# Two rows of the first chunk in banks of another ring, first reads in another order

## The chip, the cores and the metric

The kernel runs on one core of a Trainium2 chip. The metric is device time in microseconds (us) of the whole program. Engines are named as in the profile: PE is TensorE (PEld its weight loads), DVE is VectorE, ACT is ScalarE, POOL is GpSimd and SP is SyncE, which here only issues DMAs.

## The reference

One step of a decoder trunk with two layers, on 1024 prompt tokens and 8 x 4 sample tokens, 1056 in all, with a model width of 1024. The first layer is an RG-LRU block (width 1536), the second an HGRN2 block; both begin with an RMS norm and an input projection and end with an output projection and a residual. All is in float32. Cut to what the change touches:

```python
def _rmsnorm(x, gain):
    y = xf * lax.rsqrt(jnp.mean(xf * xf, axis=-1, keepdims=True) + EPS)
    return y * gain

def _lru_layer(x, g_norm, w_in, conv_w, conv_b, w_r, b_r, w_i, b_i, lam, w_out, h0, buf):
    xn = _rmsnorm(x, g_norm)
    u = xn @ w_in                                  # 1024 x 3072
    xb, gate = u[..., :W_LRU], u[..., W_LRU:]
    xc, new_buf = _causal_conv(xb, conv_w, conv_b, buf)
    h, h_last = _rg_lru(xc, w_r, b_r, w_i, b_i, lam, h0)
    y = h * silu(gate)
    return x + y @ w_out, h_last, new_buf

def _trunk(x, ...):
    x, h, bf = _lru_layer(x, ...)                  # layer 0
    x, S = _hgrn_layer(x, ...)                     # layer 1
    return _rmsnorm(x, final_gain), h, bf, S
```

## The kernel before

**Tiles.** The activations lie transposed: features on the 128 partitions, tokens along the rows. The 1056 tokens are three chunks of 352 (`CH`). A *row* of a projection is 128 output features: `product` makes it for one chunk out of eight blocks of 128 input features. A float32 product is made of three fast matmuls (`mm3`, L291 to L293): x and w are split into a rounded high part and the rest (`xh`, `xl`; `whi`, `wlo`), and hi x hi, lo x hi and hi x lo are added up in one PSUM bank. So a row of one chunk is 24 matmuls. ACT makes the high parts (L436 for weights, L956 for x), DVE or POOL subtract for the rest (L379, L957).

**Banks.** PSUM has eight banks in two rings of four: `mm` for the products of the projections, `hg` for the small matmuls beside them (gates of the recurrence L647/L651, sums and broadcasts of the norm). `next(mm)` takes the next bank of the ring, and a product that takes a bank has to wait until what lay in it has been read.

**The start.** The first six rows, three of the gate and three of the convolution branch (`items`), are computed chunk by chunk, with all their weights loaded at the start: rows one and two of the first chunk together (`pair`), then three to six. The norm of the first two chunks (`UN`) isn't applied to x: the products are made of x times the gain, and when a bank is read, L611 or L551 multiply by a broadcast of the root of the norm, `bcs[c]`. `by_token` makes that: it reads the chunk's tokens once more, with tokens on the partitions (`xt`, three reads into tiles `R`), ACT squares and sums them (L511), DVE and POOL take the root (L512, L518), DVE puts it on a diagonal (L519, L522), PE spreads it over the partitions (L524), ACT copies it (L965). Until the first data are there PE runs `WARM` small matmuls (L813).

**The order of the work.** Every operation is recorded with `fl.add`: engine, an assumed duration, what it reads and writes, a priority. `Flow.run` plans the order of each engine from these, first by list scheduling and then by `search`, which tries random changes and keeps those that make the planned end no later: `SEARCH` tries for what lies in the first 60 us or so, and then a part of that number for the whole layer. The instructions are then issued in this order, and each engine runs its own in order. `pin` fixes the order of the first DMAs: the reads with smaller numbers come first in SP's queue. The products of the projections keep their order among themselves (`main=True`); the small matmuls are put between them by the plan. The two layers are planned one after the other.

Of the kernel before, what the change touches and what calls it, by code (L numbers as in the profile page):

```python
# [19 lines left out]
ALU = mybir.AluOpType  # L20
PSUM = bass.MemoryType.PSUM
KB = 5
WARM = 32
SEARCH = 3000
NW, NXO, NRAW = 4, 3, 3
K1 = 5
NMM = 3
# [14 lines left out]
CH = 352  # L42
# [9 lines left out]
class Flow:  # L52
# [180 lines left out]
    def run(self, tries=0, first=0.0):  # L233
        self.after = [[] for _ in self.ops]
        for i, o in enumerate(self.ops):
            for d in o[3]:
                self.after[d].append(i)
        best = got = self.plan([o[4] for o in self.ops])
        for _ in range(self.TURNS):
            got = self.plan(self.back(got[2], got[4]))  # L240
            self.ends.append(got[0])
            best = min(best, got, key=lambda g: g[0])
        if tries:
            best = self.search(self.search(best, tries, first), tries // 2, 1e6)
        self.log = [(i, self.ops[i][0], best[1][i], best[2][i]) for i in best[3]]
        for i in best[3]:
            self.ops[i][2]()
# [12 lines left out]
def tile_trunk(ctx: ExitStack, tc: tile.TileContext, xT, xt, prm, hc, w0, wg, wo0, w1, wo1, s_in,  # L260
# [86 lines left out]
    with ExitStack() as l0:  # L347
# [10 lines left out]
            return cycle([(psum.tile([128, 512], F32, tag=tag, bufs=n, name=tag), (tag, i)) for i in range(n)])  # L358

        def dma(dst, src, r=(), w=(), prio=5, kb=180, q=Q):  # L360
            fl.add("SP" if q is Q else "ACT", 0.45, lambda: q.dma_start(dst, src), r, w, prio, kb * (1.0 if r or fl.exact else 0.75))

        def pin(*at):

# [79 lines left out]

            return get

        def product(w, xs, step=8, more=()):

            ps, pk = next(mm)
            n = len(xs)  # L450
            for s in range(0, n, step):
                ks = range(s, min(n, s + step))

                def emit(ks=ks):
                    for k in ks:
                        mm3(ps[:, :CH], w(k)[:2], *xs[k][:2], k == 0, k == n - 1)

                fl.add("PE", (0.484 if fl.exact else 0.48) * len(ks), emit, (*(q for k in ks for q in (*xs[k][2], *w(k)[2])), *more), (pk,), 1, main=True)
            return ps, pk

        def xcols(c):
# [41 lines left out]
        def by_token(c, prio):  # L503

            r, rk = next(nrs)
            dve(4, lambda: V.memset(r, 1.0), (), (rk,), 0)
            for i, (a, u) in enumerate(spans(CH)):
                t, tk = next(spots)
                dma(t[:u], xt[c * CH + a:c * CH + a + u], (), tk, prio, 4 * u * 0.75)
                pin((3, 8, 10)[c], i)  # L510
                act(D, lambda t=t, u=u, i=i: S.activation(junk[0][:u], t[:u], AF.Square, accum_out=r[:u, i:i + 1]), tk, (*junk[1], rk), prio, 0.06)  # L511
            dve(3, lambda: V.tensor_scalar(r[:, :3], r[:, :3], 1.0 / D, EPS, op0=ALU.mult, op1=ALU.add), (rk,), (rk,), 0)  # L512
            return spread(r, rk, next(xrs))
# [107 lines left out]
        def lru(g):  # L621
# [11 lines left out]
            for c in range(NCH):  # L633
# [5 lines left out]
                for i, hb in ((0, hbr), (1, hbi)):  # L639
                    for j in range(3):  # L640
                        m = 3 * g + j
                        ps, pk = next(hg)
                        (a, ak), (b, bk) = xpart(j, 0, c), xpart(j, 1, c)
                        u = 3 * i + j
                        fl.add("PE", 0.48, lambda ps=ps, a=a, b=b, u=u: mm3(ps[:, :CH], (gh[:, u, :], gl[:, u, :]), a, b, True, True),
                               (ak, bk, ("gh", u // 4 * 4), ("gl", u // 4 * 4)), (pk,), 0)
                        act(CH, lambda ps=ps, R=R, i=i, j=j, hb=hb, m=m: S.activation(R[:, i, j], ps[:, :CH], AF.Tanh, bias=hb[:, m:m + 1],  # L647
                                                                           scale=0.5), (pk, ("sm",)), (("R", s, i, j),), 2, 0.05)
                    ps, pk = next(hg)

                    fl.add("PE", 0.62, lambda ps=ps, i=i, c=c: T.matmul(ps[:96, :CH], gs[:, i, :], ST[:96, chunk(c)], start=True, stop=True),  # L651
                           (("gs",), *(("ST", j, c) for j in range(3))), (pk,), 0)
                    act(CH, lambda ps=ps, i=i: S.activation(td[:, i], ps[:96, :CH], AF.Tanh, bias=hbd[:96, 4 * i + g:4 * i + g + 1],
                                                            scale=0.5), (pk, ("sm",)), (("td", i),), 2, 0.05)
                    for j in range(3):
                        w = slice(32 * j, 32 * j + 32)
                        dma(R[w, i, j], td[w, i], (("td", i),), (("R", s, i, j),), 2, 45)
# [289 lines left out]
        def begin(c, first, last):  # L947

            for i in range(first, last):
                ws.append(weights(items[i][0], 1024, (0, 1, 1.2, 1.6, 1.7, 1.8)[i], V if i in VI else G, homes[i], Q if i else S, raw1[i], (-1, 0, 2, 4, 5, 7)[i]))  # L950
            for k, (x, xk) in enumerate(raw[c]):
                dma(x, xT[k][:, chunk(c)], (), (xk,), (0, 1.4, 1.9)[c])
                pin(0.001 if (c, k) < (0, 2) else (1, 6, 9)[c], k)
                if c in UN:
                    a, b = xh[k][:, chunk(c)], xl[k][:, chunk(c)]
                    act(CH, lambda x=x, a=a, k=k: S.activation(a, x, AF.Copy, scale=g0s[k]), (xk, ("g0",)), (("xh", k, c),), 1)  # L956
                    dve(CH, lambda x=x, a=a, b=b, k=k: V.scalar_tensor_tensor(b, x, g0s[k], a.bitcast(F32), op0=ALU.mult, op1=ALU.subtract),  # L957
                        (xk, ("g0",), ("xh", k, c)), (("xl", k, c),), 1, True)
                if c not in BYTOK:
                    squares(k, x, xk, accs[c], V, sqs)  # L960
            if c == 0:
                dma(hct, hc, (), (("hct",),), 2, 196)
            bc, bk = by_token(c, (1.25, 1.65, 2.0)[c]) if c in BYTOK else norm(accs[c], next(xrs))
            if c in UN:
                act(CH, lambda bc=bc: S.copy(bcs[c][0], bc), (bk,), (bcs[c][1],), 0)  # L965
            else:
                for k, (x, xk) in enumerate(raw[c]):
                    scaled_parts(c, k, x, xk, bc, bk, g0s[k], ("g0",), G if k % 4 == 3 else V)

        def products(c):  # L970
# [3 lines left out]
                    items[i][1](c, *got, bcs[0])  # L974
                order = order[2:]
            for i in order:
                items[i][1](c, *product(ws[i], xcols(c), 1, more=later[i]), *(bcs[c:c + 1] if c in UN else []))

        def pair(ws, xs):

            got = [next(mm) for _ in ws]
            for k, (a, b, ks) in enumerate(xs):
                for w, (ps, pk) in zip(ws, got):
                    fl.add("PE", 0.48, lambda ps=ps, w=w, k=k, a=a, b=b: mm3(ps[:, :CH], w(k)[:2], a, b, k == 0, k == KD - 1),
                           (*ks, *w(k)[2]), (pk,), 1, main=True)
            return got

# [933 lines left out]
```

## Time and profile before

| | |
|---|---|
| median of 3 runs | 1049.08 us (1048.25 to 1051.23) |
| the profiled execution | 1046.86 us |
| its span, first to last instruction | 1044.9 us |
| PE busy | 1030.1 us, 99% of the span |
| DVE, ACT, POOL busy | 78%, 55%, 49% |
| granted TensorE clock, mean | 0.997 |
| DMA engines' share, 10 to 20 us and 40 to 50 us | 0.97 and 0.50 |

The profile is that of one execution. Matmuls are pipelined and overlap in its rows, so the step from one start to the next is what one of them costs PE. In the list of waits, and in brackets behind a row of the timeline, stand the engine's idle time and what is taken to have ended it; the instruction named is the last that ended before, which need not be the one that was needed. In rows of windows stand the busy time of each engine with its number of records, then the granted clock, the share of the 16 DMA engines and the GB/s they moved.

### The profile page before, as it was taken

The page shows a single profiled execution, that of the slowest core. Times are in us where ns is not written, and L with a number is a line of the kernel's source. Part 1 is how long each engine was busy: PE and PEld are TensorE (multiplying, and loading weights), DVE is VectorE, ACT ScalarE, POOL GpSimd, SP SyncE. Part 2 cuts the span into 40 slices and gives each one's busy share as a digit, 9 for nine tenths or more (in the row PEclk, how much of TensorE's full clock was granted, in tenths as well). Part 3 has the DMA queues.
Part 4 walks back from the last instruction along what each step waited for, and adds up shares of the span by engine and source line. Part 5 has one row for each costly group of instructions (what it writes and reads, how often), then busy time and mean ns, then how long its engine had stood idle before and what let it go on. Part 6 is the DMA issues. An engine that isn't in the chain of part 4 may idle for free.

```text
span 1044.9 us, 25535 instructions
## 1 busy us (share of the span) xinstructions
PE 1030.1 (99%) x9810; PEld 1000.3 (96%) x9810; DVE 817.5 (78%) x1622; ACT 572.0 (55%) x1276; POOL 512.9 (49%) x596
## 2 busy tenths in 40 slices
PE   9999999999999999999999999999999999999997
PEld 9899999999999999999999999999999999999986
DVE  5889797889789679555588997988979797995436
ACT  6576746865764875334345464646463645652324
POOL 0225354454535456644527655555555555552544
PEclk9999999999999999999999999999999999999998
DMA  9701212223751686553655141423324242577204
GB/s 300 224 17 53 58 48 75 58 54 110 234 171 52 187 257 182 173 186 112 191 151 162 55 163 61 129 87 112 106 93 133 80 138 85 182 220 215 87 1 167
DMA packets 93210, 135.00 MB, mean 129 GB/s; under 512 B 11776, under 2 KB 70144, under 8 KB 93088
## 3 DMA queue, kind: packets, MB, share of 16 engines
q1 hardware_dynamic: 83296, 116.97, 36.4%
q10 hardware_dynamic: 9792, 16.40, 5.0%
q8 instruction: 77, 1.26, 0.5%
q14 instruction: 45, 0.37, 0.1%
HBM read 90.26 MB, written 38.20 MB: 123 GB/s over the span
## 4 chain that ended last, share of the span: by engine, by line
PE 66%; DVE 6%; issue 2%; DMA 1%; POOL 1%; ACT 1%; POOLq 0%; SPq 0%; DVEq 0%; ACTq 0%
PE mm L291 18%; PE mm L292 18%; PE mm L293 18%; PE hg L1161 2%; PE hg L1375 1%; PE hg L1377 1%; DVE R L1143 1%; DVE sg L1143 1%; PE hg L1419 1%; PE hg L1323 1%; DVE R L1544 1%; PE mm L1323 1%; DVE a L1343 0%; PE hg L1246 0%; PE hg L651 0%
## 5 line engine op out<-in xcount | busy, mean ns | idle before, releaser
L291 PE MATMUL mm<-xh,whi 128*128 128x352 f32 (+1 forms) x1127 | 351.7, 312 | 0.4 <-DVE k L1607 0.4
L293 PE MATMUL mm<-xh,wlo 128*128 128x352 f32 (+1 forms) x1127 | 347.6, 308 | 0.0
L292 PE MATMUL mm<-xl,whi 128*128 128x352 f32 (+1 forms) x1127 | 347.4, 308 | 0.0
L379 POOL TENSOR_TENSOR wlo<-wraw,whi 128x256 fp32r<-128x256 f32 (+3 forms) x188 | 209.1, 1128 | 191.9 <-ACT whi L1534 78.9
L291 PEld LDWEIGHTS mm<-xh,whi 128*128 128x128 f32 x1127 | 211.8, 188 | 2.7 <-DVE k L1607 1.0
L292 PEld LDWEIGHTS mm<-xl,whi 128*128 128x128 f32 x1127 | 212.2, 188 | 1.5 <-DVE xl L379 0.2
L293 PEld LDWEIGHTS mm<-xh,wlo 128*128 128x128 f32 x1127 | 212.0, 188 | 0.0
L291 PE MATMUL mm<-t,whi 128*128 128x264 f32 (+1 forms) x330 | 96.5, 292 | 0.8 <-DVE k L1607 0.8
L292 PE MATMUL mm<-t,whi 128*128 128x264 f32 (+1 forms) x330 | 94.4, 286 | 0.0
L293 PE MATMUL mm<-t,wlo 128*128 128x264 f32 (+1 forms) x330 | 94.3, 286 | 0.0
L576 DVE SCALAR_TENSOR_TENSOR k<-xb,prm_sb,k 128x352 f32<-128x352 f32 (+2 forms) x144 | 89.2, 626 | 4.4 <-ACT k L573 1.2
L379 POOL TENSOR_TENSOR wlo<-R,whi 128x256 fp32r<-128x256 f32 x70 | 66.1, 964 | 34.9 <-ACT whi L1534 19.9
L1607 DVE TENSOR_TENSOR k<-mm,k 128x264 f32<-128x264 f32 x154 | 64.0, 423 | 16.0 <-PE mm L293 14.8
L666 POOL TENSOR_TENSOR k<-X 128x352 f32<-128x352 f32 x36 | 43.0, 1199 | 59.5 <-DVE R L667 47.1
L291 PEld LDWEIGHTS mm<-t,whi 128*128 128x128 f32 x330 | 62.0, 188 | 1.6 <-DVE k L1607 1.0
L293 PEld LDWEIGHTS mm<-t,wlo 128*128 128x128 f32 x330 | 62.1, 188 | 0.0
L292 PEld LDWEIGHTS mm<-t,whi 128*128 128x128 f32 x330 | 62.1, 188 | 0.0
L436 ACT CAST whi<-wraw 128x512 fp32r<-128x512 f32 (+2 forms) x79 | 43.4, 571 | 20.0 <-PE mm L292 13.9
L291 PE MATMUL mm<-yh,whi 128*128 128x352 f32 x153 | 51.1, 334 | 0.6 <-DVE k L718 0.6
L293 PE MATMUL mm<-yh,wlo 128*128 128x352 f32 x153 | 49.4, 323 | 0.0
L647 ACT ACTIVATE R<-hg,smalls 128x352 f32<-128x352 f32 x72 | 38.2, 550 | 20.4 <-DVE R L687 11.0
L292 PE MATMUL mm<-yl,whi 128*128 128x352 f32 x153 | 49.4, 323 | 0.0
(454 smaller groups left out, 2501.5 us busy)
## 6 DMA issues: line engine op xcount, KB each, us to landing
wraw<-in_w_dram SPq DMA_DIRECT2D x52, 256.0 KB, 3.0
wraw<-in_w_dram ACTq DMA_DIRECT2D x37, 256.0 KB, 3.0
wraw<-in_wo_dram SPq DMA_DIRECT2D x34, 192.0 KB, 2.5
R<-in_w_dram ACTq DMA_DIRECT2D x17, 256.0 KB, 3.5
sg<-in_xT_dram SPq DMA_DIRECT2D x24, 176.0 KB, 4.3
si<-in_s_in_dram SPq DMA_DIRECT2D x8, 512.0 KB, 6.2
vt<-sg SPq DMA_DIRECT2D x8, 512.0 KB, 3.1
sg<-vt SPq DMA_DIRECT2D x32, 128.0 KB, 2.8
```

What stands on the lines that cost most here:

```text
L291: T.matmul(out, wh, xh, start=first, stop=False)
L292: T.matmul(out, wh, xl, start=False, stop=False)
L293: T.matmul(out, wl, xh, start=False, stop=last)
L379: emit = lambda: e.tensor_tensor(b, x, a.bitcast(F32), op=ALU.subtract)
L436: act(m, lambda hi=hi, raw=raw, m=m: S.copy(hi[:, :m], raw[:, :m]), rk, (hk,), prio)
L576: dve(u, lambda src=src, dst=dst, sh=sh, k=k: V.scalar_tensor_tensor(dst, sh(src, k), pc("cw", 12 * k + m), dst, op0=ALU.mult, op1=ALU.add ...
L647: act(CH, lambda ps=ps, R=R, i=i, j=j, hb=hb, m=m: S.activation(R[:, i, j], ps[:, :CH], AF.Tanh, bias=hb[:, m:m + 1], scale=0.5), (pk, ("s ...
L666: pool(CH, lambda x=x, a=a, b=b: G.tensor_tensor(x, a.bitcast(F32), b.bitcast(F32), op=ALU.add), (ak, bk), (xk,), 3)
L1143: dve(n // 2, lambda sv=sv, dv=dv, s=s, f=f: V.tensor_tensor(dv[:, :, s, :], sv[:, :, s, :], f, op=ALU.mult), (*sk, *gk), dk if i == o els ...
L1161: T.matmul(ps[32 * j:32 * j + 32, n * w:n * w + w], B[:, o:o + 32], q(slice(o, o + 32)), start=True, stop=True, tile_position=(0, 32 * j))
L1323: T.matmul(ps[:, n * 128:(n + 1) * 128], kt[:, 4 * i + n, :], vt[:, 4 * i + n], start=True, stop=True)
L1607: dve(QT, lambda: V.tensor_tensor(o[0], z[0], u[0], op=ALU.add), (z[1], u[1]), (o[1],), 0)
```

## The change

- Rows five and six of the first chunk take their banks from `hg` instead of `mm` (`product` gets a `ring`). All later products take the `mm` banks in turn, as before.
- The first reads are pinned in another order: row four's weights ahead of the first chunk's token reads, row six's weights ahead of the second chunk's x.
- `WARM` goes from 32 to 36, `SEARCH` from 3000 to 5000, the second part of the search from a half to a sixth of it (1500 to 833 tries).
- The planner reckons 0.482 us for three matmuls, where it had 0.48, and 0.87 or all of a first read's size, where it had 0.75.

```diff
-WARM = 32
-SEARCH = 3000
+WARM = 36
+SEARCH = 5000
...
-            best = self.search(self.search(best, tries, first), tries // 2, 1e6)
+            best = self.search(self.search(best, tries, first), tries // 6, 1e6)
...
-            fl.add("SP" if q is Q else "ACT", 0.45, lambda: q.dma_start(dst, src), r, w, prio, kb * (1.0 if r or fl.exact else 0.75))
+            fl.add("SP" if q is Q else "ACT", 0.45, lambda: q.dma_start(dst, src), r, w, prio, kb * (1.0 if r or fl.exact else 0.87))
...
-        def product(w, xs, step=8, more=()):
+        def product(w, xs, step=8, more=(), ring=None):
 
-            ps, pk = next(mm)
+            ps, pk = next(ring or mm)
...
-                fl.add("PE", (0.484 if fl.exact else 0.48) * len(ks), emit, (*(q for k in ks for q in (*xs[k][2], *w(k)[2])), *more), (pk,), 1, main=True)
+                fl.add("PE", (0.484 if fl.exact else 0.482) * len(ks), emit, (*(q for k in ks for q in (*xs[k][2], *w(k)[2])), *more), (pk,), 1, main=True)
...
-                dma(t[:u], xt[c * CH + a:c * CH + a + u], (), tk, prio, 4 * u * 0.75)
-                pin((3, 8, 10)[c], i)
+                dma(t[:u], xt[c * CH + a:c * CH + a + u], (), tk, prio, 4 * u)
+                pin((4, 8, 10)[c], i)
...
-                ws.append(weights(items[i][0], 1024, (0, 1, 1.2, 1.6, 1.7, 1.8)[i], V if i in VI else G, homes[i], Q if i else S, raw1[i], (-1, 0, 2, 4, 5, 7)[i]))
+                ws.append(weights(items[i][0], 1024, (0, 1, 1.2, 1.6, 1.7, 1.8)[i], V if i in VI else G, homes[i], Q if i else S, raw1[i], (-1, 0, 2, 3, 5, 6)[i]))
...
-                pin(0.001 if (c, k) < (0, 2) else (1, 6, 9)[c], k)
+                pin(0.001 if (c, k) < (0, 2) else (1, 7, 9)[c], k)
...
-                items[i][1](c, *product(ws[i], xcols(c), 1, more=later[i]), *(bcs[c:c + 1] if c in UN else []))
+                items[i][1](c, *product(ws[i], xcols(c), 1, later[i], None if c or i < 4 else hg), *(bcs[c:c + 1] if c in UN else []))
```

The other two places with 0.48 for three matmuls change as the first does. In what follows the instructions stand as the built programs have them, with the numbers of their tiles.

On PE, in the first chunk, before: the end of row three (`mm_160`, weights in `X`), the broadcast L524 and the beginning of row four (`mm_161`, weights in `yh0`).

```order
L291 MATMUL mm_160<-xh_109,X_144 128x352
L292 MATMUL mm_160<-xl_110,X_144 128x352
L293 MATMUL mm_160<-xh_109,X_144 128x352
L524 MATMUL hg_163<-k_87,ones_80 128x352
L291 MATMUL mm_161<-xh_95,yh0_152 128x352
L292 MATMUL mm_161<-xl_96,yh0_152 128x352
L293 MATMUL mm_161<-xh_95,yl0_155 128x352
```

And after, the end of row four, the same broadcast, and the beginning of row five (weights in `yh1`):

```order
L291 MATMUL mm_161<-xh_109,yh0_152 128x352
L292 MATMUL mm_161<-xl_110,yh0_152 128x352
L293 MATMUL mm_161<-xh_109,yl0_155 128x352
L524 MATMUL hg_163<-k_87,ones_80 128x352
L291 MATMUL hg_165<-xh_95,yh1_153 128x352
L292 MATMUL hg_165<-xl_96,yh1_153 128x352
L293 MATMUL hg_165<-xh_95,yl1_156 128x352
```

The broadcast has moved behind row four, and row five goes to `hg_165` (row six to `hg_162`); before, row five went to `mm_158`, the bank of row one.

In SP's queue, the first reads, before: weights in `a`, `ST` and `wraw`, the first chunk's tokens in `R` (from `in_xt`), and the beginning of the second chunk's x in `sg` (from `in_xT`).

```order
L361 DMA a_114<-in_w0_dram 128x512
L361 DMA a_115<-in_w0_dram 128x512
L361 DMA R_73<-in_xt_dram 128x1024 x2
L361 DMA R_73<-in_xt_dram 96x1024
L361 DMA a_115<-in_w0_dram 128x512
L361 DMA ST_145<-in_w0_dram 128x512
L361 DMA wraw_121<-in_w0_dram 128x512
L361 DMA wraw_122<-in_w0_dram 128x512
L361 DMA sg_146<-in_xT_dram 128x352
```

And after, from the same read on:

```order
L361 DMA a_114<-in_w0_dram 128x512
L361 DMA a_115<-in_w0_dram 128x512 x2
L361 DMA ST_145<-in_w0_dram 128x512
L361 DMA R_73<-in_xt_dram 128x1024 x2
L361 DMA R_73<-in_xt_dram 96x1024
L361 DMA wraw_121<-in_w0_dram 128x512
L361 DMA wraw_122<-in_w0_dram 128x512
L361 DMA ST_145<-in_w0_dram 128x512
L361 DMA sg_146<-in_xT_dram 128x352
```

Row four's weights (the second read into `a_115` and the first into `ST_145`) have moved ahead of the tokens, and the first half of row six's (the second into `ST_145`) ahead of the second chunk's x. Further on, not shown, the second chunk's token reads stand behind all of the third chunk's x and the reads of `gs`, `hct` and one block into `xo`; before, they stood among and ahead of these.

On DVE, in the second chunk, before: the third chunk's root (L512) and its diagonal (L519, L522; `nr0`), and the first bank that is read, L611 on `mm_158`.

```order
L512 TENSOR_SCALAR nr0_132<-nr0_132 128x3
L494 MEMSET nr1_133 128x4
L582 TENSOR_TENSOR X_144<-k_87,X_144 128x352
L576 SCALAR_TENSOR_TENSOR k_87<-xb_2_136,prm_sb_74,k_87 128x352
L519 TENSOR_TENSOR k_87<-ident_75,nr0_132 128x256
L522 TENSOR_SCALAR k_87<-ident_75,nr0_132 128x96
L494 MEMSET nr0_132 128x4
L860 RECIPROCAL smalls_84<-smalls_84 128x8
L582 TENSOR_TENSOR X_144<-k_87,X_144 128x352
L860 TENSOR_TENSOR smalls_84<-smalls_84 128x8 x4
L860 TENSOR_SCALAR smalls_84<-smalls_84 128x8
L611 TENSOR_TENSOR sg_147<-mm_158,xo_1_138 128x352
```

And after, the second chunk's root and diagonal (`nr1`), the third chunk's, and L611 on the bank of the second chunk's first row, which is `mm_158` now:

```order
L512 TENSOR_SCALAR nr1_133<-nr1_133 128x3
L582 TENSOR_TENSOR X_144<-k_87,X_144 128x352 x2
L519 TENSOR_TENSOR k_87<-ident_75,nr1_133 128x256
L522 TENSOR_SCALAR k_87<-ident_75,nr1_133 128x96
L494 MEMSET nr1_133 128x4
L512 TENSOR_SCALAR nr0_132<-nr0_132 128x3
L519 TENSOR_TENSOR k_87<-ident_75,nr0_132 128x256
L611 TENSOR_TENSOR sg_148<-mm_158,xo_1_138 128x352
L611 TENSOR_TENSOR sg_147<-mm_160,xo_1_138 128x352
```

L611 follows L519 directly. On PE the second chunk's L524 has moved towards that chunk's fifth row, which takes the bank of its first: 38 rows of PE's order lay between them before, 13 now. The last 5,159 instructions of PE, which begin shortly before the second layer, have the same order before and after.

More of the change, by code (lines that the diff above doesn't have):

```diff
@@ L644, in lru @@
                         u = 3 * i + j
-                        fl.add("PE", 0.48, lambda ps=ps, a=a, b=b, u=u: mm3(ps[:, :CH], (gh[:, u, :], gl[:, u, :]), a, b, True, True),
+                        fl.add("PE", 0.482, lambda ps=ps, a=a, b=b, u=u: mm3(ps[:, :CH], (gh[:, u, :], gl[:, u, :]), a, b, True, True),
                                (ak, bk, ("gh", u // 4 * 4), ("gl", u // 4 * 4)), (pk,), 0)
@@ L983, in pair @@
                 for w, (ps, pk) in zip(ws, got):
-                    fl.add("PE", 0.48, lambda ps=ps, w=w, k=k, a=a, b=b: mm3(ps[:, :CH], w(k)[:2], a, b, k == 0, k == KD - 1),
+                    fl.add("PE", 0.482, lambda ps=ps, w=w, k=k, a=a, b=b: mm3(ps[:, :CH], w(k)[:2], a, b, k == 0, k == KD - 1),
                            (*ks, *w(k)[2]), (pk,), 1, main=True)
```

## The prediction

> **What bounds the kernel now.** I read the page's head first, then the list of waits of TensorE, then the engine timelines at the places that the waits name.
>
> ```profile
> span 1044.9 us, 25535 instructions
> PE 1030.1 (99%) x9810; PEld 1000.3 (96%) x9810; DVE 817.5 (78%) x1622; ACT 572.0 (55%) x1276; POOL 512.9 (49%) x596
> ...
> PE mm L291 <- DVE nr L506: 2.1, 1, 2.1
> PE hg L1215 <- DVE R L1143: 1.6, 1, 1.6
> PE mm L291 <- DVE k L1607: 1.1, 2, 0.8
> PE hg L813 <- DVE nr L506: 1.0, 1, 1.0
> PE hg L1789 <- DVE sg L1779: 0.8, 1, 0.8
> PE mm L291 <- DVE k L718: 0.6, 1, 0.6
> PE hg L291 <- ACT R L647: 0.3, 1, 0.3
> ...
> PE hg L524 <- DVE k L522: 0.2, 1, 0.2
> ```
>
> PE (TensorE) is busy for 1030.1 of 1044.9 us, so the time changes only by work added to PE and by its waits. In each row of waits the first number is the total. Those of the first layer are 2.1 (fifth row of the first chunk), 0.2 (the broadcast of L524), 0.6 and 0.3 (L718, L647, late in that layer); 1.0 is the start. The order of PE's last 5,159 instructions, the whole second layer among them, is the same before and after, so I leave 1.6, 1.1 and 0.8 as they are. What the change can win is thus a little over 3 us, 0.3% of the time, which is also about what a measurement of this kernel can tell from no change.
>
> The start and the two waits in the timeline of PE (start, duration, instruction):
>
> ```profile
> 1.03 9.04 PE L813 MATMUL hg<-ones 128*128 128x128 f32 x64 [1.03 <-DVE nr L506]
> 9.82 0.41 PE L291 MATMUL mm<-xh,whi 128*128 128x352 f32 x1
> ...
> 21.34 0.32 PE L293 MATMUL mm<-xh,X 128*128 128x352 f32 x1
> 21.82 0.86 PE L524 MATMUL hg<-k,ones 128*128 128x352 f32 x2 [0.16 <-DVE k L522]
> 22.25 0.59 PE L291 MATMUL mm<-xh,yh 128*128 128x352 f32 x1
> 22.67 0.32 PE L292 MATMUL mm<-xl,yh 128*128 128x352 f32 x1
> ...
> 26.19 0.32 PE L293 MATMUL mm<-xh,yl 128*128 128x352 f32 x1
> 28.57 0.42 PE L291 MATMUL mm<-xh,yh 128*128 128x352 f32 x1 [2.06 <-DVE nr L506]
> 28.83 0.32 PE L292 MATMUL mm<-xl,yh 128*128 128x352 f32 x1
> ...
> 36.36 0.32 PE L291 MATMUL mm<-xh,X 128*128 128x352 f32 x1
> ```
>
> Records of PE overlap, so I work with the step from one start to the next. The wait at 28.57 is named after a memset, but what ends it is the emptying of the first bank:
>
> ```profile
> 22.78 3.47 ACT L956 ACTIVATE xh<-sg,g 128x352 fp32r<-128x352 f32 x7
> ...
> 27.18 0.44 ACT L965 COPY xo<-hg 128x352 f32<-128x352 f32 x1
> ...
> 28.00 0.96 DVE L611 TENSOR_TENSOR sg<-mm,xo 128x352 f32<-128x352 f32 x2
> ```
>
> The four `mm` banks hold rows one to four. The fifth needs bank one, whose L611 needs the copied broadcast of L965, which stands behind seven L956 on ACT; L611 starts at 28.00, and PE 0.57 later.
>
> **The change part by part.**
>
> *Two rows in the other ring.* The fifth and sixth row no longer wait for L611. The steps give the price: from 26.19 to 28.83 are 2.64 us for two steps. An ordinary step is 0.16 (48.05 to 48.21 in the next fence), so two take 0.32, and 2.32 us go. What is late next is the bank of chunk two's first row. It starts near 34.6 (below) and finds bank one emptied if L611 ends by then; in after's order L611 stands behind all eight of chunk two's xl. L611's 28.00 leaves 6 us for that. The reads of rows five's and six's weights have as many bytes ahead of them as before, or fewer.
>
> *The broadcast after the fourth row.* L524 waited for its input; an undisturbed one tells its own cost:
>
> ```profile
> 48.05 0.32 PE L292 MATMUL mm<-xl,yh 128*128 128x352 f32 x1
> 48.21 0.32 PE L293 MATMUL mm<-xh,yl 128*128 128x352 f32 x1
> 48.37 0.75 PE L524 MATMUL hg<-k,ones 128*128 128x352 f32 x2
> 48.69 0.59 PE L291 MATMUL hg<-X,gh 128*128 128x352 f32 x1
> 49.12 0.32 PE L292 MATMUL hg<-X,gh 128*128 128x352 f32 x1
> ```
>
> From the last matmul ahead of it to the second behind it: 49.12 - 48.21 = 0.91. At the first broadcast it is 22.67 - 21.34 = 1.33. The difference, 0.42 us, goes if the input is there in time. It comes later now: two reads of 256 KB (row four's weights, 128x512 of four bytes) stand ahead of the token reads, 0.524 MB.
>
> ```profile
> 21.50 0.26 DVE L522 TENSOR_SCALAR k<-ident,nr 128x96 f32<-128x96 f32 x1
> 10.00:26.50 16.50, 16.34 (x99) 15.57 (x97) 10.07 (x23) 12.93 (x28) 0.86 (x1) 1.00 1.01 331
> ```
>
> The DMA engines were full there (share 1.01) at 331 GB/s, so 1.6 us later: 21.76 becomes 23.4. PE reaches L524 near 26.2, so 2.8 us cover it; without that cover the 0.42 would come back and grow.
>
> *Four more warm-up matmuls.* Each is two records. The mean of 9.04 us over 64 would be 0.141 a record and 1.13 us for eight. But the records are not alike:
>
> ```profile
> 1.00:5.00 4.00, 3.97 (x21) 1.00 0.81 253
> 5.00:9.00 4.00, 4.00 (x38) 1.00 1.00 324
> ```
>
> Early ones take about 0.2 us, later ones 4.00/38 = 0.105 to 4.00/36 = 0.111 (two records may only reach in). The added ones come at the end, so they cost eight times the later price: 0.84 to 0.89, I take 0.87. The column PEclk says 1.00 in both windows and would not have told this. The Trainium skill, "TensorE: Matmul & The Clock Gate", Part 1: The HAM clock gate, says that the array starts at half rate and is released after some 3.4 us of work, so that matmuls past that buy nothing more; the records of this trace agree. By that rule the sum takes 0.87 as well, and by the mean alone 1.13. Is this on the path? PE did not wait ahead of 9.82, so the first product stood behind the warm-up, and its inputs were ready:
>
> ```profile
> 8.13 1.08 DVE L957 SCALAR_TENSOR_TENSOR xl<-sg,g,xh 128x352 fp32r<-128x352 f32 x2 [0.49 <-ACT xh L956]
> ```
>
> The first two xl are done at 9.21. So all of it counts: three of the four end before the first product (9.82 + 0.65 = 10.47), and one stands behind its first six matmuls.
>
> *The new weave.* Search length, planned rates and pins issue nothing themselves, but every engine's order in the first layer is new. Two places could get waits. The first is chunk two's fifth row, which reuses the bank of its first. Before, 38 rows of PE's order lay from that chunk's L524 to it; now 13, L524 and twelve matmuls. The chain between is L524, L965, L611. DVE has L519 for chunk three ahead of that L611, and this needs the last token reads:
>
> ```profile
> 45.72 1.06 ACT L511 ACTIVATE R<-R 96x1024 f32<-96x1024 f32 x1 [0.68 <-DMA R<-in_xt_dram]
> ...
> 49.46 0.43 DVE L519 TENSOR_TENSOR k<-ident,nr 128x256 f32<-128x256 f32 x1 [0.24 <-POOL nr L518]
> ...
> 51.37 0.52 DVE L611 TENSOR_TENSOR sg<-mm,xo 128x352 f32<-128x352 f32 x1
> 40.00:50.00 10.00, 10.00 (x63) 9.79 (x62) 8.99 (x41) 5.16 (x11) 2.89 (x6) 1.00 0.50 112
> ```
>
> When does PE arrive? From 9.82 to the end of row three are 11.68 us (21.34 + 0.16), row four is 24 steps of 0.161, L524 adds 0.59 (0.91 less two steps), rows five and six are 48 steps: 10.47 + 0.22 + 11.68 + 3.86 + 0.59 + 7.73 = 34.55 for chunk two, against 36.36, which is the same gain of 1.8 by another way. 93 steps on, L524 starts at 49.5, and the fifth row is due 0.59 + 12 x 0.16 later, at 52.0. L524's 0.75, L965's 0.44 and L611's 0.52 end at 51.2, with hand-overs of 0.05 (28.52 to 28.57) to 0.2 each near 51.5: no wait. By way of L519, L611 has to start at 51.4, so L519 may be 1.5 us later than 49.46. The token reads of chunk two now have 616 KB more ahead (one x block, gs, hct, xo), 0.63 MB, 1.9 us at 331 GB/s; those of chunk three go into the same tiles and follow. But between 40 and 50 us the DMA engines were half idle (share 0.50), which can take up much of it. So L519 is late by 0 to 2 us, the wait 0 to 0.5.
>
> The second place is the rest of the layer: the 0.6 and 0.3 may go, or others of that size come, -0.9 to +0.9. For both together I take +0.3, the smallest wait that such a weave shows (L647), and keep -0.9 and +1.4 as ends.
>
> **Sum**, against the profiled execution of 1046.86 us (span 1044.9 and 2.0 around it): -2.32 - 0.42 + 0.87 + 0.3 = -1.57, so 1045.3. The median of the runs, 1049.08, lies 2.2 above that execution; taken off it, the forecast is 1047.5 us. The ends of the unknown terms give 1046.3 and 1048.6.
>
> **The rivals.**
>
> *A: the wait is longer in ordinary runs.* The first 40 us are read at the full rate of the DMA engines, and a run in which reads come later lengthens the fifth row's wait, while the new order has 2.8 us of cover at L524 and more at the banks. If the 2.2 us between the profiled execution and the median lie there, they go too: 1049.08 - 1.57 - 2.2 = 1045.3. For it: share 1.01 and more, and runs from 1048.25 to 1051.23. Against it: nothing shows where the 2.2 us lie. Faster by over 0.3%, chance 0.25.
>
> *B: chunk three's token reads hold up the banks of chunk two.* If L519 comes d later than 49.46, PE waits d - 1.5. At d = 3.4 the gain is gone; at d = 6.5 the kernel is 3.15 us slower; at d = 8 the time is 1049.08 - 1.87 + 6.5 = 1053.7. For it: three L611 stand right behind that L519, and SP's queue is in order, so a late store ahead of these reads delays them all. Against it: 1.9 us is what the bytes give. Chance 0.13, for the side of slower. By the same page's rule an idle of PE of about 3.4 us puts the clock back to half, which as an estimate from it would add some 1.7 us at d = 8; no wait in this trace is that long.
>
> *C: the gain is given back.* The shift arrives earlier at rows whose DVE and ACT work is no earlier, and waits like L718's and L647's grow by as much: 1049.1. Against it: these two are all that 500 us of such weave show. Chance 0.17.
>
> **How the numbers follow.** The forecast itself has 0.45. Forecast and C lie within 0.3% (3.15 us): 0.62. Faster 0.25 (A), slower 0.13 (B). The range takes in the forecast's ends and C, most of A with its scatter of about a microsecond between runs, and the beginning of B: 1044.6 to 1050.6.
>
> **What would show it.** Right: no wait on PE between 21 and 36 us, the first product near 10.5, chunk two's first row near 34.6, L519 of chunk three before 51.0 and no wait at the fifth row near 52. The forecast is wrong if PE waits for DVE near 52 or 63 us for over 1 us, if the first-layer waits beyond 60 us exceed 2 us, or if the profiled execution gains 1.6 us and the median another amount.

## The result, and the profile after

| | before | after |
|---|---|---|
| median, runs of one job | 1048.25 us (7 runs) | 1042.99 us (1042.54 to 1045.69, 7 runs) |
| ratio | | 0.9954, 95% interval 0.9939 to 0.997 |
| the profiled execution | 1046.86 us | 1045.33 us |
| its span | 1044.9 us | 1043.5 us |

The kernel became faster by 5.3 us, 0.5%. That lies outside the predicted range, and "faster by over 0.3%" had a chance of 0.25 there. The two profiled executions differ by only 1.5 us, close to what the sum gave (1.57).

Head and list of PE's waits of the changed kernel (total, times, longest):

```profile
span 1043.5 us, 25547 instructions
PE mm L291 <- DVE k L1607: 2.3, 5, 0.8
PE mm L291 <- DVE xb L718: 1.2, 2, 0.7
PE hg L813 <- DVE nr L506: 1.0, 1, 1.0
PE hg L1789 <- DVE sg L1779: 0.6, 1, 0.6
```

The two longest waits of before are gone: the fifth row's 2.1 and, which the prediction did not have, the 1.6 of L1215 behind VectorE's L1143 in the second layer; so are three of 0.2 to 0.3. L718 and L1607 have grown by 0.6 and 1.2. PE's timeline at the places of the prediction, and then DVE's:

```profile
1.04 9.85 PE L813 MATMUL hg<-ones 128*128 128x128 f32 x70 [1.04 <-DVE nr L506]
10.65 0.41 PE L291 MATMUL mm<-xh,whi 128*128 128x352 f32 x1
...
26.23 0.32 PE L293 MATMUL mm<-xh,yl 128*128 128x352 f32 x1
26.39 0.75 PE L524 MATMUL hg<-k,ones 128*128 128x352 f32 x2
26.71 0.59 PE L291 MATMUL hg<-xh,yh 128*128 128x352 f32 x1
27.14 0.32 PE L292 MATMUL hg<-xl,yh 128*128 128x352 f32 x1
...
34.68 0.32 PE L291 MATMUL mm<-xh,X 128*128 128x352 f32 x1
```

```profile
30.73 0.52 DVE L611 TENSOR_TENSOR sg<-mm,xo 128x352 f32<-128x352 f32 x1
...
48.58 0.42 DVE L519 TENSOR_TENSOR k<-ident,nr 128x256 f32<-128x256 f32 x1 [0.96 <-POOL nr L518]
50.95 1.39 DVE L611 TENSOR_TENSOR sg<-mm,xo 128x352 f32<-128x352 f32 x3 [1.94 <-ACT xo L965]
```

The front does what was forecast: L524 and rows five and six follow without a wait, and chunk two starts at 34.68 (forecast 34.55). So the question is where the other 3 to 4 us of the medians come from.

A table by stretch helps to see it. A row's eight steps of three matmuls each have one L293; I took the starts of these from each timeline, in order, without those of the gates (`hg<-X,gl`). 48 steps are the first chunk's six rows, and those from 840 to 1000 lie around the change of layers, at about 472 to 558 us. Times in us, one profiled execution each; the kernels below before and after are the experiments of the next section.

| | start to step 48 | 48 to 840 | 840 to 1000 | 1000 to end |
|---|---|---|---|---|
| before | 36.7 | 435.8 | 85.7 | 486.7 |
| before, again | 39.1 | 436.3 | 85.9 | 486.9 |
| after | 35.0 | 436.8 | 83.9 | 487.9 |
| after, again | 36.0 | 436.2 | 83.9 | 487.2 |
| ring_same_plan | 34.9 | 436.3 | 84.9 | 487.6 |
| fill_wait | 37.6 | 435.8 | 84.8 | 487.4 |
| second_new | 38.7 | 435.8 | 83.8 | 484.0 |
| second_old | 35.5 | 436.3 | 84.9 | 485.9 |
| ring_second | 35.1 | 437.6 | 83.8 | 486.3 |
| no_ring | 37.0 | 436.7 | 83.9 | 487.4 |
| ring_replanned | 37.1 | 440.9 | 86.1 | 487.1 |
| warm_same_plan | 34.1 | 436.0 | 83.9 | 486.3 |
| warm28 | 33.2 | 436.6 | 83.9 | 488.3 |
| warm24 | 33.2 | 435.9 | 83.9 | 488.2 |

Two columns tell the kernels apart: the front, and the 160 steps of the third. The last column spreads over 4 us and does not follow the edits.

### The profile page after: what moved, and what is told of

Same layout as the page of the kernel before. It is cut to its first block, busy times and chain, and to the rows that moved or that the text cites. A ratio compares the mean times of both kernels' runs of the same rounds, so it can differ in the third digit from the quotient of the medians.

```text
span 1043.5 us, 25547 instructions
## 1 busy us (share of the span) xinstructions
PE 1031.7 (99%) x9818; PEld 1002.2 (96%) x9818; DVE 817.2 (78%) x1622; ACT 573.0 (55%) x1276; POOL 513.3 (49%) x596
## 4 chain that ended last, share of the span: by engine, by line
PE 90%; DVE 7%; issue 1%; ACT 0%; POOL 0%; DMA 0%; POOLq 0%; DVEq 0%; ACTq 0%
PE mm L291 25%; PE mm L293 25%; PE mm L292 24%; PE hg L1161 2%; PE hg L291 1%; PE hg L292 1%; PE hg L293 1%; PE hg L1375 1%; PE hg L651 1%; PE hg L1377 1%; PE hg L813 1%; DVE a L1343 1%; DVE sg L1143 1%; DVE R L1143 1%; PE hg L1419 1%
## 5 line engine op out<-in xcount | busy, mean ns | idle before, releaser
L293 PE MATMUL mm<-xh,wlo 128*128 128x352 f32 (+1 forms) x1127 | 347.5, 308 | 0.0
L379 POOL TENSOR_TENSOR wlo<-wraw,whi 128x256 fp32r<-128x256 f32 (+3 forms) x188 | 207.7, 1122 | 181.4 <-ACT whi L1534 73.9
L293 PEld LDWEIGHTS mm<-xh,wlo 128*128 128x128 f32 x1127 | 211.9, 188 | 0.0
L293 PE MATMUL mm<-t,wlo 128*128 128x264 f32 (+1 forms) x330 | 94.3, 286 | 0.0
L379 POOL TENSOR_TENSOR wlo<-R,whi 128x256 fp32r<-128x256 f32 x70 | 64.1, 936 | 46.4 <-ACT whi L1534 29.6
L1607 DVE TENSOR_TENSOR k<-mm,k 128x264 f32<-128x264 f32 x154 | 64.0, 422 | 15.8 <-PE mm L293 15.2
L293 PEld LDWEIGHTS mm<-t,wlo 128*128 128x128 f32 x330 | 62.2, 188 | 0.0
L1534 ACT CAST whi<-wraw 128x512 fp32r<-128x512 f32 x56 | 34.5, 616 | 28.4 <-DVE wraw L1544 12.7
L293 PE MATMUL mm<-yh,wlo 128*128 128x352 f32 x153 | 49.4, 323 | 0.0
```

What stands on the lines that cost most here:

```text
L293: T.matmul(out, wl, xh, start=False, stop=last)
L379: emit = lambda: e.tensor_tensor(b, x, a.bitcast(F32), op=ALU.subtract)
L1534: act(512, lambda: S.copy(hi, raw), (rk,), (hk,), 2)
L1607: dve(QT, lambda: V.tensor_tensor(o[0], z[0], u[0], op=ALU.add), (z[1], u[1]), (o[1],), 0)
```

## The experiments

All were timed in five rounds, in three jobs with kernel before beside them (medians of before: 1047.74, 1048.16 and 1047.78 us).

### First job: is it the front wait, later waits, or PE's own pace?

**before_again and after_again**: both kernels unchanged, for a second profile of each.

> The kernel before, unchanged, for a second profiled execution. Theory F (front): in ordinary runs the fifth row's wait is longer than the 2.06 us of the first profile; an execution of 1048 to 1050 us then shows 3.5 to 6 us of idle PE ahead of the fifth row and the same waits elsewhere. Theory L (later): that wait stays at 2.0 to 2.4 us whatever the execution's time, and the rest lies in waits beyond 60 us. Theory N (nothing to do with PE's waits): PE's idle time is 14.5 to 15.5 us as before and the executions differ in PE's busy time. Time: 1047 to 1051 us, ratio 0.999 to 1.001.

> The changed kernel, unchanged, for a second profiled execution. All theories: 1042.5 to 1045.7 us, ratio 0.994 to 0.997. Theory F: PE has no wait between 20 and 60 us in it either, and chunk two begins at 34.7 us. Theory L: an execution of about 1043 us has some 2 us less of PE's waits in the second layer than the profiled one of 1045.33 (there L1607 2.3 us).

Measured: before_again 1048.49 us, ratio 1.0005 (0.9995 to 1.0016); after_again 1044.28 us, ratio 0.9969 (0.9959 to 0.9979), without a wait between 20 and 60 us. The second profile of before is 3.3 us longer than the first. Of this 2.4 us lie in the front: the first product starts 0.68 later (10.50 for 9.82), and most of the rest comes behind the fifth row's wait. First this wait, then the steps behind it in PE's timeline of before_again:

```profile
29.42 0.43 PE L291 MATMUL mm<-xh,yh 128*128 128x352 f32 x1 [2.02 <-DVE nr L506]
29.68 0.41 PE L292 MATMUL mm<-xl,yh 128*128 128x352 f32 x1
29.89 0.49 PE L293 MATMUL mm<-xh,yl 128*128 128x352 f32 x1
30.18 0.49 PE L291 MATMUL mm<-xh,yh 128*128 128x352 f32 x1
30.48 0.49 PE L292 MATMUL mm<-xl,yh 128*128 128x352 f32 x1
...
33.32 0.32 PE L293 MATMUL mm<-xh,yl 128*128 128x352 f32 x1
```

Windows of the same execution (us, busy PE, number of records, then the granted clock, DMA share and GB/s):

```profile
29.00:30.00 1.00, 0.58 (x3) 0.89 0.96 346
30.00:31.00 1.00, 1.00 (x5) 0.50 1.03 374
31.00:32.00 1.00, 1.00 (x5) 0.50 1.00 393
32.00:33.00 1.00, 1.00 (x5) 0.50 1.21 332
33.00:34.00 1.00, 1.00 (x8) 0.90 0.93 154
```

And the first profile of before behind its wait of 2.06 us:

```profile
29.00:30.00 1.00, 1.00 (x8) 1.00 1.02 379
30.00:31.00 1.00, 1.00 (x8) 1.00 1.04 405
```

The wait has the same length in both, so theory F falls. But in before_again the clock falls to half for about 3.4 us behind it: the step is 0.29 instead of 0.16, and step 48 starts 9.67 us behind the fifth row instead of 8.11, about 1.6 us more. The prediction was built on an execution in which that did not happen. The mean granted clock of each run tells roughly how often it does: of 63 runs of before in the three jobs 22 had 0.994 or 0.995 (median 1048.66 us) and 41 had 0.996 or 0.997 (median 1047.53 us). 3.4 us at half clock in 1046 us lower the mean by 0.0016, about that step. The count is rough because the clock is at half at the end of every span too, for 5.2 to 8.9 us in these profiles; an execution of second_new below has the fall and a mean of 0.996. Of the changed kernel's 15 runs none was under 0.996. PE's idle time is 15.0 us as theory N said, and its busy time, which contains the slow steps, is 3.1 us longer (1033.2 for 1030.1).

The Trainium skill, "TensorE: Matmul & The Clock Gate", Part 1: The HAM clock gate, puts the fall behind an idle window of about 3.4 us and calls the window free-running. The length of the fall agrees; the wait that brings it does not: here 2.02 us were enough in one execution and 2.06 us not in another. The measurement decides.

A phase that differs between executions fits both, and the traces show one. In the records of the clock of all fourteen profiles, the changes lie whole multiples of 3.41 us apart (in before_again at 5.89, 29.78 and 33.20; in before at 4.47 and 1038.70, which is 303 of them). In before_again the whole wait, 27.40 to 29.42, lies in the one interval that ends with the fall at 29.78. In before such an interval ends at 28.36, inside the wait, so only 1.84 us of it lie in one interval, and nothing fell. The two other falls that the profiles show, in second_new and ring_replanned below, have their whole wait in one interval as well. If that is what decides, a wait of 2.05 us lies wholly in one interval in (3.41 - 2.05) / 3.41 = 40% of the phases, an estimate from these numbers; 22 of 63 runs are 35%. No experiment set the phase.

**ring_same_plan**: the banks alone, every engine's order as in before.

```diff
 at = {4: side[3], 5: side[0]}.get(i) if c == 0 else None   # side: the four hg banks
-items[i][1](c, *product(ws[i], xcols(c), 1, more=later[i]), ...)
+items[i][1](c, *product(ws[i], xcols(c), 1, later[i], at), ...)
```

> The kernel before with its own order of all instructions, and only the two PSUM banks exchanged: the products of rows five and six of the first chunk go to the two hg banks. Row five then starts right behind row four, near 26.4 us in place of 28.57, as its weights allow (their second half is ready at 28.1, needed at 28.3). Theory F: the whole gain of the change and more, 3 to 6 us (1042.5 to 1045.5), as no warm-up is added. Theory L: 2.0 to 2.5 us (1045.8 to 1046.3 against 1048.25). If the gain is under 1.5 us, the gain of the change comes from the other edits or the new weave.

Measured: 1046.56 us, ratio 0.9991 (0.9982 to 1.0001), a gain of 0.9 us by the ratio, less than either theory gave; the interval includes no change. The profile shows no wait at the fifth row and the front of the changed kernel (34.9 us), with four warm-ups fewer and the wait at L524 still there. So the banks alone give that front, but not the whole gain: something else is in the changed kernel.

**warm_same_plan**: the changed kernel's order, with four of its 36 warm-ups issued as nothing.

> The changed kernel with its own order of all instructions, without four of its 36 warm-up matmuls. If eight records at full clock are on the path, the first product starts at 9.8 us in place of 10.65 and chunk two 0.8 to 0.9 us earlier, and the kernel is 0.9 us faster than the changed one (1042.1 against 1043.0), unless a wait takes its place. If the inputs or a later wait bound that stretch, the time is the same as the changed one's, with new idle of 0.9 us ahead of a product below 60 us.

Measured: 1042.76 us, ratio 0.996 (0.9947 to 0.9974). The first product starts at 9.98 us, 0.67 and 1.71 earlier than in the two profiles of the changed kernel. Of the 1.71, about 1.0 goes to a later start of full speed (6.97 us for 4.79, at 0.21 in place of 0.11 us a record; more of this under warm24). So by the profiles the added warm-ups cost about the 0.65 that was forecast; the medians are too close to tell.

### Second job: the clock, and the second layer's order

**fill_wait**: before's order, with PE kept at work while the fifth row waits.

```diff
 def emit(ks=ks):
+    for _ in range(fill if 0 in ks else 0):      # fill = 8 for the fifth row of chunk one
+        T.matmul(warm[:, :128], ones, ones, start=True, stop=True)
     for k in ks:
```

> The kernel before in its own order, with eight more matmuls of ones put directly ahead of the fifth row's first product, into the bank of the warm-ups, so that PE works through most of the 2.0 us in which it waited there (eight at about 0.22 us are 1.8 us). Theory H (the wait costs its 2.0 us and, in part of the executions, 1.5 us more because the clock falls to half behind it): the wait itself is not shortened, but no slice of 28 to 36 us has a clock of 0.5; the median falls by 0.5 to 1.5 us against before, to about 0.999, and the executions lie closer together. Theory C (the fall of the clock behind the wait is rare, the spread of before comes from the start): median within 0.3 us of before.

Measured: 1046.41 us, ratio 0.9989 (0.9978 to 0.9999). The fifth row starts no earlier (29.54 us), nothing of the work went away and 16 records were added, and the kernel is faster, if only just clear of the noise. Its timeline and windows there:

```profile
27.38 1.95 PE L456 MATMUL hg<-ones 128*128 128x128 f32 x16
29.54 0.43 PE L291 MATMUL mm<-xh,yh 128*128 128x352 f32 x1 [0.21 <-DVE nr L508]
```

```profile
28.00:30.00 2.00, 1.79 (x15) 1.00 1.02 367
30.00:32.00 2.00, 2.00 (x14) 1.00 1.05 389
```

All eleven runs have a clock of 0.996 or 0.997, and they spread over 2.6 us where before spreads over 5.0. Theory H holds; the gain is 1.2 us by the ratio, within its 0.5 to 1.5, and 1.75 by the medians.

**second_new and second_old**: the second layer's order of the one kernel under the first layer of the other. The planner gets the other kernel's start times (shortened here), number of tries and divisor there; the orders of all engines in the second layer are then those of the other kernel, as the traces confirm. What differs there between before and after are VectorE, ScalarE and SyncE: of VectorE's last 800 instructions 177 stand in another place.

```diff
-fl = Flow(side=0.4, busy={e: max(0.0, t - last["PE"]) for e, t in last.items()})
+fl = Flow(side=0.4, busy={"PE": 0.0, "DVE": 0.0, "ACT": 1.3048, "POOL": 4.1756, "SP": 0.2697})  # second_new
...
-            best = self.search(self.search(best, tries, first), tries // 2, 1e6)
+            best = self.search(self.search(best, tries, first), tries // (6 if self.exact else 2), 1e6)
...
-            fl.run(SEARCH, 60.0)
+            fl.run(5000, 60.0)
```

> The kernel before, with its first layer as it was, and in the second layer the order of all engines that the changed kernel has (the planner's start and number of tries there are set to the changed kernel's values; PE's order stays as it is, DVE's, ScalarE's and SyncE's change). Theory L (the 1.6 us wait of PE for VectorE's work at line 1143, near 540 us, goes because the second layer was planned again): that wait is gone, the stretch from the 840th to the 1000th main product is 83.9 us instead of 85.7, and the median is 1.8 us lower, ratio 0.9983. Rival E (the wait depends on when the first layer ends on each engine): the wait stays and the time is that of before within 0.4 us.

> The changed kernel, with the second layer in the order of the kernel before on all engines. Theory L: the wait near 540 us comes back with 1.6 us, and of the changed kernel's gain of 4 us against before 1.8 us are lost: ratio about 0.998 instead of 0.9965. Rival E: no such wait, ratio as the changed kernel's, 0.996 to 0.997.

Measured: second_new 1044.29 us, ratio 0.9965 (0.9954 to 0.9975); second_old 1044.52 us, ratio 0.9969 (0.9956 to 0.9981). In second_new the list of waits still has the fifth row, the windows still have the half clock behind it, and L1215 is not in the list any more:

```profile
PE mm L291 <- DVE nr L506: 2.1, 1, 2.1
```

```profile
30.00:31.00 1.00, 1.00 (x6) 0.50 1.02 398
```

The row is back in second_old's list of waits, with half its size:

```profile
PE hg L1215 <- DVE R L1143: 0.8, 1, 0.8
```

So the wait belongs to the second layer's order: it stands in all six profiles with before's order there (0.7 to 1.6 us) and in none of the eight with the changed kernel's. Rival E's mechanism falls. The price of the wait is 0.9 to 2.3 us by the third column (84.8 to 86.1 against 83.8 to 83.9). How it comes about is seen in DVE's and PE's timelines, first before:

```profile
534.83 1.87 DVE L1475 TENSOR_TENSOR sg<-sg 128x264 f32<-128x264 f32 x2
...
536.80 0.67 DVE L1143 TENSOR_TENSOR R<-R,sg 128x512 f32<-128x512 f32 x1
537.40 0.67 DVE L1143 TENSOR_TENSOR sg<-sg 128x512 f32<-128x512 f32 x1
538.11 1.67 DVE L1143 TENSOR_TENSOR a<-sg 128x512 f32<-128x512 f32 x1
539.70 0.68 DVE L1143 TENSOR_TENSOR R<-R,sg 128x512 f32<-128x512 f32 x1
538.20 0.76 PE L1161 MATMUL hg<-R,sg 128*32 128x32 f32 x64
540.52 0.69 PE L1215 MATMUL hg<-R,a 128*16 128x16 f32 x64 [1.56 <-DVE R L1143]
```

and after:

```profile
533.45 1.19 DVE L1143 TENSOR_TENSOR sg<-sg 128x512 f32<-128x512 f32 x1 [0.42 <-PE hg L1161]
534.56 1.78 DVE L1143 TENSOR_TENSOR R<-R,sg 128x512 f32<-128x512 f32 x1
536.26 0.68 DVE L1143 TENSOR_TENSOR a<-sg 128x512 f32<-128x512 f32 x1
536.87 0.68 DVE L1143 TENSOR_TENSOR R<-R,sg 128x512 f32<-128x512 f32 x1
537.38 0.76 PE L1161 MATMUL hg<-R,sg 128*32 128x32 f32 x64
537.99 0.69 PE L1215 MATMUL hg<-R,a 128*16 128x16 f32 x64
```

Before, the four L1143 start 1.4 us ahead of PE's L1161 (536.80 to 538.20), behind L1475 and L379 work. After, they start 3.9 us ahead (533.45 to 537.38) and are done when PE gets to L1215. PE's own order is the same in both. The sizes of the two medians fit less well: second_new gained 3.7 us by its ratio where 1.8 was expected, and second_old lost nothing against after_again (0.9969 both), as rival E had it. In second_new's one profile 2.7 us of the gain lie in the last column, which this order has at 484.0 to 488.3 us. A good part of that spread is PE's wait for VectorE's L1607, here in second_new and then in warm28, the two ends of the column:

```profile
PE mm L291 <- DVE k L1607: 0.2, 1, 0.2
PE mm L291 <- DVE k L1607: 3.1, 5, 1.0
```

That makes 2.9 of the 4.3 us between them, in two executions whose engines have the same order there. Why VectorE comes later in one than in the other was not found.

**warm28**: as warm_same_plan, with 28 warm-ups.

> The changed kernel's order of everything, with 28 warm-up matmuls instead of 36. If PE's warm-ups and not the loads set the first product's start, it starts earlier than with 32 (9.98 us): eight at 0.22 us are 1.8 us less than the changed kernel, at most down to where the inputs are there, about 9.2 us, so the median is about 1.5 to 2 us below the changed kernel's, ratio 0.995. Rival: the clock is released later or falls behind the idle time ahead of the first product, and the first products run at half speed: no gain over 32 warm-ups (0.996).

Measured: 1042.69 us, ratio 0.9943 (0.9929 to 0.9958), the lowest of all kernels, though its interval overlaps the changed kernel's. The first product starts at 9.15, right behind the last warm-up.

### Third job: do the two causes make up the gain?

**ring_second**: ring_same_plan with second_new's second layer. **no_ring**: the changed kernel with `None` for the ring of rows five and six, planned again. **ring_replanned**: before with `None if c or i < 4 else hg` as that ring and nothing else, planned again.

> The kernel before with two parts of the change alone: the banks of the fifth and sixth row of chunk one in the other ring (with the first layer's order as it was), and the second layer in the changed kernel's order. Theory T (two independent causes, the fifth-row wait with the half clock behind it and the wait near 540 us, make up the whole gain): no wait for the fifth row, no clock of 0.5, no wait at line 1143 near 540 us; the median is that of the changed kernel, ratio 0.995 to 0.9965. Rival O (the changed kernel's own order of the first reads matters too): at least 1 us above the changed kernel, ratio 0.9975 or more.

> The changed kernel without its new banks, planned again: the fifth and sixth row of chunk one take the ring that all rows take; the second layer comes out in the changed kernel's order. Theory T: the fifth row waits 2 us or more again, in a part of the executions with a clock of 0.5 behind it, and the wait near 540 us stays away: ratio as with the second layer's order alone, 0.9965 (0.996 to 0.9975). Rival O: the changed kernel's order of the first reads moves the early wait away by itself, ratio as the changed kernel's or lower, at most 0.9955.

> The kernel before with the new banks for the fifth and sixth row alone, planned again with before's own constants, first reads and tries; the second layer comes out in before's order. Theory T: no wait for the fifth row, no clock of 0.5, the wait near 540 us stays with 0.7 to 1.6 us: ratio 0.998 to 0.999. Rival O: the planner uses the new banks for more than the fifth row's wait, ratio at most 0.9965.

Measured: ring_second 1044.8 us, ratio 0.997 (0.9958 to 0.9982); no_ring 1046.08 us, 0.9981 (0.9972 to 0.9989); ring_replanned 1051.67 us, 1.0035 (1.0023 to 1.0047).

ring_second has neither wait and the third column of the changed kernel, and its interval overlaps both of the changed kernel's. Two of its five runs have a clock of 0.995, as has one of the eleven of ring_same_plan; the profiles of the two show no cause. Its ratio lies between the two expectations. It gains 3.1 us, about what after_again gains (3.2) and less than the 4.8 of the first job: that the two causes give all of the gain is not shown. In no_ring the fifth row waits again, but less than expected:

```profile
28.90 0.43 PE L291 MATMUL mm<-xh,yh 128*128 128x352 f32 x1 [1.10 <-DVE sg L611]
```

Here L611 really ended last, 1.0 us of the old wait has gone by the order of the first reads and of the front alone, and none of the eleven runs has a clock under 0.996. Rival O is thus right for half of the wait, and Theory T for the other half. The ratio, 0.9981, is above what either gave, and no experiment tells why. ring_replanned refuted both. The fifth row's wait is gone, and the planner, with the old constants, put three others in its place; two of them in the timeline, and windows behind the second:

```profile
36.63 0.43 PE L291 MATMUL mm<-xh,X 128*128 128x352 f32 x1 [1.55 <-DVE sg L611]
...
113.42 0.43 PE L291 MATMUL mm<-xh,whi 128*128 128x352 f32 x1 [2.23 <-DVE sg L611]
```

```profile
113.00:114.00 1.00, 0.58 (x3) 0.94 0.26 98
114.00:115.00 1.00, 1.00 (x6) 0.50 0.00 0
115.00:116.00 1.00, 1.00 (x5) 0.50 0.18 45
...
117.00:118.00 1.00, 1.00 (x7) 0.86 0.00 0
```

The same banks give 0.9991 in before's order, with an interval that includes 1, and 1.0035 in the order that the planner makes for them. A wait of 2.23 us in another place, with the DMA engines nearly idle, has the half clock behind it too, so the full DMA engines of the front are not needed for it.

**warm24**: 24 warm-ups in the changed kernel's order.

> The changed kernel's order of everything, with 24 warm-up matmuls instead of 36 (28 gave 0.9943, and its first product, at 9.15 us, still followed its last warm-up by 0.03 us). If the loads are there earlier, the first product starts near 8.3 us and the ratio falls by up to 0.0009 to 0.9935; if the loads set it at about 9 us, the ratio stays 0.994. Rival: the clock falls to half behind the idle time ahead of the first product, and the kernel loses 1.5 us: 0.9955.

Measured: 1043.58 us, ratio 0.9959 (0.9947 to 0.9971): no lower than 28. Its first product started at 9.15 as with 28, though it has eight records fewer. The warm-ups' pace explains that. Windows of PE's warm-ups in warm28:

```profile
5.00:7.00 2.00, 2.00 (x21) 1.00 1.05 359
```

and in after_again:

```profile
5.00:7.00 2.00, 2.00 (x12) 1.00 1.05 360
7.00:9.00 2.00, 2.00 (x20) 1.00 0.99 319
```

From about 5 us on the warm-ups run at the fast pace in the one, from 7 us on in the other; warm24's profile changes pace at 6.8 us. So the start depends on when the fast pace begins as much as on the count, and 24 and 28 could not be told apart by these runs.

## Why the prediction was wrong

**The front: right.** The fifth row's 2.32 us and L524's 0.42 are gone (26.23 to 27.14 is the 0.91 of an undisturbed broadcast). The first product came 0.83 us later than before, against 0.65 forecast for three of the four warm-ups, and chunk two 1.68 earlier than 36.36, against 1.81. One link of the old wait was read short: L965 ended at 27.62, and until 28.00 L611 stood behind two L379 on VectorE; the price does not change by it.

**"I leave 1.6, 1.1 and 0.8 as they are": the first step that failed.** It took the second layer's waits as fixed because PE's order there is the same. But the second layer is planned again too, with another number of tries, and the wait at L1215 hung on where VectorE's L1143 stands in VectorE's order. It went, 1.8 us in the third column, and second_new shows that the second layer's order alone makes the kernel faster (0.9965, 0.9954 to 0.9975). With it fell "a little over 3 us" as the most that the change can win.

**"2.32 us go": the term that was mis-sized.** It came from an execution in which the clock stayed up behind the wait. In others about 1.6 us are lost to half clock behind it; at roughly 22 of 63 that is 0.5 us on the mean.

**Rival A** had the place right and the cause wrong. It asked whether the 2.2 us between profile and median lie in the fifth row's wait; the wait was 2.0 to 2.1 us in three profiles, and what differed was the clock behind it and at the start. The sentence on an idle of 3.4 us stood under rival B, for reads that come 8 us late; by its measure the wait of 2.06 that the list already showed was too short to matter, and in part of the executions it was not.

**Rival B** did not come: L519 of chunk three started at 48.58, 0.9 us earlier than before and not up to 2 later, and L611 at 50.95, in time. **Rival C** is seen in part: in the profiled execution the stretch from step 48 to 840 is 1.0 us longer (L718 from 0.6 to 1.2), inside the ends of -0.9 and +1.4; in the second pair of profiles it is equal (436.3 and 436.2).

**The sum**: the profiled gain of 1.5 agrees with the forecast 1.57 by luck. It is front -1.7, first layer +1.0, the stretch with L1215 -1.8, the rest of the second layer +1.2, and 0.2 outside the span. The forecast was also taken off a median of three runs, 1049.08; with seven runs before has 1048.25, which is 0.8 of the 4.5 us between forecast and result. The prediction's own sign for being wrong was met: "the profiled execution gains 1.6 us and the median another amount".

**What stays open**: the medians gain 5.3 and, in the later job, about 3.5 us. Front 1.7, half clock 0.5 and L1215 0.9 to 2.3 make 3.1 to 4.5, of which the first layer gives back 1.0 in one pair of profiles and nothing in the other. The parts do not add up either: by the ratios the banks alone gain 0.9 us, the second layer's order alone 3.7, the changed kernel with the old second layer 3.2, and banks and second layer together 3.1, each give or take about 1 us. So that the two waits go, and what they go with, is shown; how the gain of the medians is shared between them is not. Nor was it found why VectorE's L1607 comes later in some executions than in others of equal orders.

## What to carry to other kernels

When a change goes through a planner, compare the order of every engine in every stage, not that of the engine at the limit alone: a wait of PE can hang on where another engine's work stands, as at L1215. Price a wait of PE with what may follow it: here about 2 us of idle cost another 1.6 us of half clock in part of the executions. So look at the granted clock of several executions, and try filling a wait that can't be removed. An edit that does no harm in a fixed order can lose when the planner makes a new order from it, so try it both ways.

## What was not expected of the hardware

- The clock fell to half for about 3.4 us behind waits of 2.02, 2.15 and 2.23 us, and not behind one of 2.06 us in another execution of the same kernel, nor, in these profiles, behind any of 1.6 us or less. The three falls had the whole wait in one of the intervals of 3.41 us on which the clock changed; the wait of 2.06 lay across the end of one.
- The warm-up's change from 0.21 to 0.11 us a record came between 4.4 and 7.0 us of the span in executions of nearly the same start, worth up to 1.2 us by an estimate (twelve records of 0.21 in those 2.6 us, each 0.1 too long); the clock column shows 1.00 through all of it, because the records of the clock begin only at that change.
